# Bias rows reversed by a diagonal DMA, late probabilities scaled on either engine, longer GpSimd memsets: one layer of a streaming encoder

## The chip, the cores and the metric

The kernel runs on one core of one Trainium2 chip. The core has five engines that run side by side and meet through semaphores: TensorE (PE in the profile; PEld is its weight load), VectorE (DVE), ScalarE (ACT), GpSimd (POOL) and SyncE (SP), which here issues the DMAs. Each engine works through its own instructions strictly in order. The metric is the device time of one execution in microseconds, given as the median of several runs.

## The reference

One layer of an encoder runs on 2048 new frames of a prompt and on 64 frames of a running stream, with rows of 1024 numbers, all in 32-bit floats. Half of the width is chunked attention in 8 heads of 64, the other half a gated linear recurrence in 4 heads of 128.

```python
def band_attention(q, k, v, rel, valid, rel_bias):
    idx = jnp.clip(rel, -REL_CLIP, REL_CLIP) + REL_CLIP
    bias = rel_bias[:, idx].astype(jnp.float32)
    s = jnp.einsum('bnqhd,bnkhd->bnhqk', q, k).astype(jnp.float32) * ATTN_SCALE + bias
    s = jnp.where(valid[None, :, None], s, NEG_INF)
    p = jax.nn.softmax(s, axis=-1).astype(v.dtype)
    return jnp.einsum('bnhqk,bnkhd->bnqhd', p, v)

def mixer_layer(x, ln_g, w_in, lb, norm_g, w_out, attn_fn, s0):
    B, T, _ = x.shape
    aq, ak, av, ag, hq, hf, hi, hg = jnp.split(rms_norm(x, ln_g) @ w_in, SPLITS, axis=-1)
    heads = lambda a: a.reshape(B, T, H_A, DH_A)
    k = heads(ak)
    v = heads(av)
    o_a = attn_fn(heads(aq), k, v).reshape(B, T, W_A) * jax.nn.silu(ag)
    o_b, S = hgrn2_branch(hq, hf, hi, hg, lb, norm_g, s0)
    y = x + jnp.concatenate([o_a, o_b], axis=-1) @ w_out
    return y, k, v, S
```

The bias depends only on the distance between query and key, clipped to 128 either way. For 128 queries against 640 keys the matrix of biases therefore has one constant part (384 keys, all further than 128 back) and one part of 256 keys whose rows are the same list of 383 numbers, each row shifted by one against the row above.

## The kernel before

The frames are handled in four superblocks (`SUPER`) of 512, 576, 512 and 512 tokens; the second has the 64 frames of the running stream. In each superblock 32 projections of 128 columns run (`JOBS`), each as 24 matmuls on high and low halves of the operands. The heads hang on these: a pair of attention heads needs its projections pq, pk, pv, pg, a recurrent head hq, hf, hi, hg. After the last superblock the output projection follows (`steps`), with seven products of half-size blocks for each 256 rows.

The order of all instructions is made when the program is built. A class `Plan` keeps a clock for every engine; `Queue` charges each instruction with a cost in ns as it is issued; generators (threads) yield a time, an engine with a time, or a condition, and are resumed when the plan's clock says so, those of lower priority number first. `yield "D", t` means: go on when time t has come and VectorE's line in the plan is less than 600 ns long. Tokens (`tk[...]`) stand for buffers. `C.pick(t, D=..., A=...)` names the engine on which an operation of the given cost would end first. A DMA on SyncE is charged 420 ns of issue, 520 ns until it moves, its bytes at 370 GB/s behind the DMAs before it, and 2000 ns until it has landed; `C.dma()` adds 100.

Three places matter here.

*The breath.* Where GpSimd gets a third instruction in a row while its line in the plan is not empty, `Queue` puts a memset of the tile `C.breath` ahead of it. In the kernel before this tile has one element per partition.

*The bias rows,* `load_bias`. One tile `bias` of 128 x 2 x 640 (two heads of a pair) exists; the pair's scores are added to it by VectorE. In superblocks 1 to 3 it is loaded from a copy in DRAM (`biasd`). In superblock 0 it is built, once for each of the four pairs: a DMA loads a window `win` in which partition i holds the 256 numbers from place i of the list on (into the tile `ck`), a second DMA loads the far value; VectorE fills the 384 constant columns; TensorE multiplies with `flip`, a matrix with ones on the other diagonal, which turns the order of the 128 partitions round; VectorE takes the product out of the bank `g` with a factor of -1; two memsets mask the corners; a DMA stores the result to `biasd`. `d.bias_at` is the planned time from which scores of the pair may go.

*The probabilities,* `softmax_exp`. ScalarE exponentiates a row block of scores and sums it, VectorE takes the reciprocal, and the block is scaled by it: on VectorE, but on ScalarE once "parts" is in `have`. That is set in `out_rows_g`, when the recurrences of the last superblock are done and the output projection has room to begin, so it concerns the last scores alone.

TensorE then transposes the scaled blocks; ScalarE copies them out as high halves, VectorE makes the low halves (`ph`), and TensorE multiplies them with v (`pv`).

Of the kernel before, what the change touches and what calls it, by code (L numbers as in the profile page):

```python
# [8 lines left out]
F32 = mybir.dt.float32  # L9
# [3 lines left out]
ALU = mybir.AluOpType  # L13
# [4 lines left out]
P = 128  # L18
D = 1024
# [353 lines left out]
def hymba_step(  # L373
# [24 lines left out]
    C = Plan()  # L398
    act, dve, pool, pe, sp = (Queue(C, e, x) for e, x in (("A", nc.scalar), ("D", nc.vector), ("P", nc.gpsimd),
                                                          ("T", nc.tensor), ("S", nc.sync)))  # L400
# [4 lines left out]
    cst = ctx.enter_context(tc.tile_pool(name="cst", bufs=1))  # L405
    wk = ctx.enter_context(tc.tile_pool(name="wk", bufs=2))
    dr = ctx.enter_context(tc.tile_pool(name="dr", bufs=1, space=DRAM))
# [5 lines left out]
    def T(pool_, shape, dt, tag, **kw):  # L413
        uid[0] += 1
        C.name(homes.get(id(pool_), ""), tag, kw.get("bufs") or 1, f"{tag}_{uid[0]}")
        return pool_.tile(list(shape), dt, tag=tag, name=f"{tag}_{uid[0]}", **kw)

    def psum(tag, shape=(P, 512), bufs=1):
        return T(ps, shape, F32, tag, bufs=bufs)
# [22 lines left out]
    def mm32(out, w, x):  # L442
        pe.matmul(out, w, x, start=True, stop=True)

    tk = {k: Tok(C, n) for k, n in dict(acc=2, s_ps=1, tr=2, pv=1, g=1, pr=PRB, ph=2, sig=2, vT=2, mixa=2,
                                     w=WBUFS, raw=RAWB, xn=XNB, kv=1, q=1, sga=2, bias=1, gf=1, gi=1, gg=1,
                                     ck=1, slot=4, x4=0, x5=0, rec=1).items()}
# [1 line left out]

    ident = T(cst, [P, P], F32, "ident")  # L450
    make_identity(nc, ident)
    flip = T(cst, [P, P], F32, "flip")
    ones = T(cst, [P, P], F32R, "ones")
    mask = T(cst, [P, P], U32, "mask")
    eps_t = T(cst, [P, 1], F32, "eps")
    one_t = T(cst, [P, 1], F32, "one")
    C.breath = T(cst, [P, 1], F32, "breath")
    reset = T(cst, [P, 512], F32, "reset")
    asb = [T(cst, [P, 4, P], F32, f"asb{i}") for i in range(2)]
    g_norm = T(cst, [P, NHB], F32, "gnorm")  # L460
# [5 lines left out]
    have = set()  # L466

    def constants():
        pool.memset(eps_t, EPS)
        pool.memset(one_t, 1.0)  # L470
        maskf = asb[0][:, 0]
        pool.memset(maskf, 1.0)
        dve.tensor_copy(ones, maskf)
        pool.memset(flip, 1.0)
        pool.affine_select(out=flip, in_=flip, pattern=[[1, P]], compare_op=ALU.is_equal, fill=0.0,
                           base=-(P - 1), channel_multiplier=1)
        pool.affine_select(out=maskf, in_=maskf, pattern=[[1, P]], compare_op=ALU.is_ge, fill=0.0,
                           base=0, channel_multiplier=-1)
        dve.tensor_copy(mask, maskf)
        pool.memset(reset, 1.0)  # L480
        pool.memset(reset.rearrange("p (b t) -> p b t", t=32)[:, :, 0:1], 0.0)
        pool.memset(asb[0], 0.0)
# [333 lines left out]
    def load_bias(sb, p, d):  # L816
        yield from tk["bias"].get()
        nb = d.bias = T(wk, [P, 2, 640], F32, "bias", bufs=1)
        if sb:
            sp.dma_start(nb, biasd[p])  # L820
            d.bias_at = C.dma(655)
            return
        yield from tk["ck"].get()
        win = T(wk, [P, 4, P], F32, "ck", bufs=1).rearrange("p (h a) c -> p h (a c)", h=2)
        sp.dma_start(win, bass.AP(rel_rev.tensor, 2 * p * 383, [[1, P], [383, 2], [1, 256]]))
        far = T(wk, [P, 2], F32, "far", bufs=1)
        sp.dma_start(far, bass.AP(rel_rev.tensor, 2 * p * 383, [[0, P], [383, 2]]))
        t = C.dma(400)
        yield "D", t
        for h in range(2):  # L830
            dve.tensor_scalar(nb[:, h, 0:384], reset[:, :384], 0.0, far[:, h : h + 1], ALU.mult, ALU.subtract)
        C.dve(600)
        yield from tk["g"].get()
        pw = psum("g")
        pe.matmul(pw, flip, win.rearrange("p h c -> p (h c)"), start=True, stop=True)
        tk["ck"].put()
        t = C.pe()
        yield "D", t
        dve.tensor_scalar(nb[:, :, 384:640], pw.rearrange("p (h c) -> p h c", h=2), -1.0, None, ALU.mult)
        tk["g"].put(1, C.dve())  # L840
        dve.memset(nb[64:128, :, 0:64], BIG)
        dve.memset(nb[0:64, :, 576:640], BIG)
        t = C.dve(900, t)
        d.bias_at = t
        yield t
        sp.dma_start(biasd[p], nb)
        C.dma(655)
# [38 lines left out]
    def pair_jobs(sb, p):  # L886
# [10 lines left out]
        def open_():  # L897

            yield from tk["kv"].get()
            d.kd = T(pa, [P, 2, WIN + NMAX], F32R, "kd")  # L900
            d.v = T(pa, [P, 9, 4, 64], F32R, "v")
            d.q = T(pa, [P, 2, QW], F32R, "q")
            if sb:
                cd = carry[sb - 1][p]
                sp.dma_start(f32(d.kd[:, :, 0:512]), cd[:, 0:2, :])
                sp.dma_start(f32(d.v[:, 0:4].rearrange("p t s d -> p (t s d)")),
                             cd[:, 2:4, :].rearrange("p a c -> p (a c)"))
                d.k_t = d.v_t = C.dma(1024)
            C.spawn(load_bias(sb, p, d), 1)
            if smp:  # L910
                pool.memset(f32(d.v[DEC:, 4 + WIN // P]), 0.0)
                C.spawn(sample_cache(d), 1)
# [98 lines left out]
    def softmax_rows(d, h, qc, spans, bcol, nk, out):  # L1011

        yield lambda: d.q_n >= qc + P and d.k_n >= qc + P and d.bias_at is not None
        yield max(d.q_t, d.k_t, d.bias_at) + 300.0
        yield from tk["s_ps"].get()
        yield from tk["pr"].get()
        sps = s_ps()
        for part in (d.q, ql):
            for i, (k0, kn) in enumerate(spans):
                mm(sps[:, i, :kn], part[:, h, qc : qc + P], d.kd[:, h, k0 : k0 + kn], kn,  # L1020
                   start=part is d.q, stop=part is ql)
        t = C.pe()
        yield "D", t
        s = T(wk, [P, 640], F32, "pr", bufs=PRB)
        nm = T(wk, [P, 2], F32, "nm", bufs=4)
        ns, kn = len(spans), spans[0][1]
        dve.tensor_tensor_reduce(
            s[:, :nk].rearrange("p (a c) -> p a c", a=ns), sps[:, :ns, :kn],
            d.bias[:, h, bcol : bcol + nk].rearrange("p (a c) -> p a c", a=ns),
            1.0, 3e38, ALU.add, ALU.min, nm[:, 0:1])  # L1030
        t = C.dve(nk + 80, t)
        tk["s_ps"].put(1, t)
        d.left -= 1
        if d.left == 0:
            if d.sb == len(SUPER) - 1 and d.p == NPAIR - 1:
                have.add("scores")
                tk["x4"].put()
            tk["bias"].put()
        yield "A", t
        yield from softmax_exp(s, nm, nk, out, t)  # L1040

    def softmax_exp(s, nm, nk, out, t):
        sm = T(wk, [P, 1], F32, "sm", bufs=4)
        act.activation(s[:, :nk], s[:, :nk], AF.Exp, bias=nm[:, 0:1], scale=-1.0, accum_out=sm)
        t = C.act(nk + 300, t)
        yield "D", t
        dve.reciprocal(sm, sm)
        t = C.dve()
        if "parts" in have:
            yield "A", t  # L1050
            act.activation(s[:, :nk], s[:, :nk], AF.Copy, scale=sm)
            t = C.act()
        else:
            dve.tensor_scalar(s[:, :nk], s[:, :nk], sm, None, ALU.mult)
            t = C.dve()
        out.append((s, t))
# [184 lines left out]
    def sample_a(d, c0, marks):  # L1241
# [41 lines left out]
        yield "A", t  # L1283
        out = []
        yield from softmax_exp(s, nm, 576, out, t)
        pr, t = out[0]
        yield lambda: marks[-1]["pv"] and turn["ph"] == turn["given"]
# [749 lines left out]
    def program():  # L2037


        dve.memset(g_in, 0.0)  # L2040
        constants()
        kroom = f32(T(pa, [P, 2, WIN + NMAX], F32R, "kd")).rearrange("p a c -> p (a c)")
        vroom = f32(T(pa, [P, 9, 4, 64], F32R, "v")).rearrange("p t s d -> p (t s d)")
# [252 lines left out]
```

## Time and profile before

| | us |
|---|---|
| median of 3 runs | 1261.63 |
| lowest, highest | 1260.84, 1261.96 |
| the profiled execution, its own time | 1260.86 |
| its span, first to last instruction | 1259.0 |
| in this span: ScalarE's wait for projections (vT, sig) | 95.5 and 73.3 |
| GpSimd's longest wait (mixa for VectorE) | 259.6 |
| HBM traffic | 215 GB/s over the span |

Most of the span is projection: the groups of matmuls with more time than all others are these (columns: line, engine and operation, output and inputs, shapes, count, then busy us and mean ns of one, then the idle time just before them).

```profile
L266 PE MATMUL acc<-xh,w 128*128 128x512 f32 (+2 forms) x2720 | 568.4, 348 | 1.0 <-ACT sig L266 0.8
L266 PE MATMUL acc<-xl,w 128*128 128x512 f32 (+2 forms) x1360 | 297.4, 348 | 0.0
L266 PE MATMUL pv<-ph,v 128*128 128x256 f32 (+2 forms) x344 | 97.2, 373 | 3.1 <-DVE ph L266 2.4
```

All instructions carry line 266, because a helper records them; groups are told apart by the names of their tiles. Durations of matmuls overlap, so busy time is their union and not count times mean. A view by stretches gives the busy time of every engine in each stretch of the span; the timeline gives instructions in order of time, with their start, length and, in brackets, how long the engine had been idle before and what ended that.

### The profile page before, as it was taken

What the parts mean: (1) busy time and instruction counts of PE and PEld (TensorE: products, weight loads), DVE (VectorE), ACT (ScalarE), POOL (GpSimd) and SP (SyncE); (2) the same over time, 40 slices, a digit from 0 to 9 for tenths busy, and PEclk for the clock granted to TensorE, in tenths of its full rate; (3) what the DMA queues carried; (4) which work ended last, traced back from release to release, by engine and by line L of the source; (5) the groups of instructions that cost most, each with busy time, mean ns of one, the idle gap of its engine ahead of it and who ended that gap; (6) DMA issues with size and microseconds to landing.
All of it is one profiled execution on the core that took longest, in us unless ns stands there. A gap on an engine that the chain in (4) does not pass through costs nothing. (4 is left out here: it accounts for less than half of the span.)

```text
span 1259.0 us, 22201 instructions
## 1 busy us (share of the span) xinstructions
PE 1238.8 (98%) x8120; PEld 1081.6 (86%) x8120; DVE 891.9 (71%) x1854; ACT 706.9 (56%) x1548; POOL 379.9 (30%) x703
## 2 busy tenths in 40 slices
PE   9999999999999999999999999999999999999997
PEld 8788887999999999998888888998888888788786
DVE  7786968766857678686584849783838574578886
ACT  6453546665656557575565656764636454753443
POOL 7766655111120210202533634110101104451110
PEclk9999999999999999999999999999999999999999
DMA  7887787645354554636879597646454657886331
GB/s 288 301 288 244 247 282 281 219 168 202 138 188 142 181 200 144 216 125 236 272 248 303 206 364 254 220 164 210 144 212 136 222 178 279 324 277 203 126 134 67
DMA packets 94830, 271.72 MB, mean 216 GB/s; under 512 B 10305, under 2 KB 43073, under 8 KB 77058
## 3 DMA queue, kind: packets, MB, share of 16 engines
q1 hardware_dynamic: 94722, 270.31, 61.4%
q8 instruction: 64, 1.05, 0.3%
q14 instruction: 44, 0.36, 0.1%
HBM read 186.66 MB, written 83.62 MB: 215 GB/s over the span
## 5 line engine op out<-in xcount | busy, mean ns | idle before, releaser
L266 PE MATMUL acc<-xh,w 128*128 128x512 f32 (+2 forms) x2720 | 568.4, 348 | 1.0 <-ACT sig L266 0.8
L266 PEld LDWEIGHTS acc<-xh,w 128*128 128x128 f32 x2720 | 436.7, 189 | 51.7 <-issue 1.4
L266 PE MATMUL acc<-xl,w 128*128 128x512 f32 (+2 forms) x1360 | 297.4, 348 | 0.0
L266 PEld LDWEIGHTS acc<-xl,w 128*128 128x128 f32 x1360 | 219.3, 189 | 24.9 <-issue 0.5
L266 POOL TENSOR_TENSOR mixa<-mixa,sga 128x256 f32<-128x256 f32 (+1 forms) x36 | 29.8, 828 | 334.8 <-DVE mixa L266 259.6
L266 DVE CUSTOM_DVE_ANT_0 pr<-s,bias 128x640 f32<-128x640 f32 (+5 forms) x144 | 100.7, 703 | 34.5 <-PE s L266 33.9
L266 ACT ACTIVATE pr<-pr,nm 128x640 f32<-128x640 f32 (+4 forms) x132 | 100.7, 763 | 39.0 <-DVE nm L266 37.9
L266 ACT CAST ph<-tr 128x512 fp32r<-128x512 f32 (+3 forms) x176 | 88.1, 507 | 59.7 <-PE tr L266 27.9
L266 POOL TENSOR_TENSOR w<-wraw,w 128x256 fp32r<-128x256 f32 x120 | 105.3, 906 | 46.9 <-DVE w L266 25.9
L266 DVE TENSOR_TENSOR ph<-tr,ph 128x512 fp32r<-128x512 f32 (+3 forms) x176 | 101.1, 589 | 10.0 <-ACT ph L266 8.8
L266 PE MATMUL pv<-ph,v 128*128 128x256 f32 (+2 forms) x344 | 97.2, 373 | 3.1 <-DVE ph L266 2.4
L266 PE MATMUL tr<-ident,pr 128*128 128x128 f32 x580 | 91.2, 273 | 2.4 <-DVE pr L266 1.2
L266 PEld LDWEIGHTS tr<-ident,pr 128*128 128x128 f32 x580 | 70.4, 140 | 16.6 <-issue 3.8
L266 ACT ACTIVATE sig<-acc 128x256 f32<-128x256 f32 (+2 forms) x86 | 42.7, 497 | 73.6 <-PE acc L266 73.3
L266 ACT COPY vT<-acc 128x512 f32<-128x512 f32 (+2 forms) x64 | 31.3, 488 | 71.2 <-PE acc L266 71.1
L266 DVE TENSOR_SCALAR pr<-pr,sm 128x640 f32<-128x640 f32 (+3 forms) x124 | 67.9, 547 | 4.4
L266 DVE TENSOR_TENSOR mixa<-mixa,pv 64x256 f32<-64x256 f32 (+1 forms) x144 | 56.8, 394 | 18.9 <-ACT mixa L266 14.7
L266 PEld LDWEIGHTS pv<-ph,v 128*128 128x128 f32 x344 | 57.4, 190 | 10.3 <-issue 2.0
L266 ACT ACTIVATE sig<-sig 128x512 f32<-128x512 f32 (+2 forms) x109 | 57.3, 528 | 10.0 <-DVE gk L266 7.3
L266 PE MATMUL s<-kd,q 128*128 128x320 f32 (+3 forms) x232 | 56.9, 315 | 0.2
L266 POOL TENSOR_TENSOR xn<-wraw,xn 128x256 fp32r<-128x256 f32 x48 | 37.8, 803 | 62.2 <-ACT xn L266 62.1
L266 PE MATMUL s<-kd,ql 128*128 128x320 f32 (+3 forms) x232 | 55.6, 309 | 0.0
(319 smaller groups left out, 2064.5 us busy)
## 6 DMA issues: line engine op xcount, KB each, us to landing
w<-wd SPq DMA_DIRECT2D x96, 1024.0 KB, 5.1
wd<-w SPq DMA_DIRECT2D x32, 1024.0 KB, 7.6
wraw<-in_w_in_dram SPq DMA_DIRECT2D x30, 512.0 KB, 5.5
wod<-xn SPq DMA_DIRECT2D x28, 512.0 KB, 5.0
xn<-in_x_prompt_dram SPq DMA_DIRECT2D x23, 512.0 KB, 5.5
bias<-biasd SPq DMA_DIRECT2D x12, 640.0 KB, 7.5
carry<-kd SPq DMA_DIRECT2D x12, 512.0 KB, 8.0
carry<-v SPq DMA_DIRECT2D x12, 512.0 KB, 5.2
```

What stands on the lines that cost most here:

```text
L266: r = f(*args, **kw)
```

## The change

The tile `flip`, its memset and its selection on GpSimd go. The tile `breath` grows from one element per partition to 128.

In `load_bias` the window, the matmul, the bank `g` and the tile `ck` go. In their place a DRAM tile `rel{p}` of 2 x 128 x 383 is filled by one DMA from DRAM to DRAM that repeats each of the two lists of 383 numbers 128 times. When the plan's clock says that it has landed, a second DMA reads it back into columns 384 to 640 of the bias tile with a step of 382 from partition to partition, so that each partition starts one place earlier in the list: that is the reversed order. VectorE then negates these columns in place. The constant columns are filled between the two.

In `softmax_exp` the late blocks go to ScalarE only where `C.pick` finds that it would end there sooner than on VectorE.

```diff
-    flip = T(cst, [P, P], F32, "flip")
...
-    C.breath = T(cst, [P, 1], F32, "breath")
+    C.breath = T(cst, [P, P], F32, "breath")
...
-        pool.memset(flip, 1.0)
-        pool.affine_select(out=flip, in_=flip, pattern=[[1, P]], compare_op=ALU.is_equal, fill=0.0,
-                           base=-(P - 1), channel_multiplier=1)
...
-        yield from tk["ck"].get()
-        win = T(wk, [P, 4, P], F32, "ck", bufs=1).rearrange("p (h a) c -> p h (a c)", h=2)
-        sp.dma_start(win, bass.AP(rel_rev.tensor, 2 * p * 383, [[1, P], [383, 2], [1, 256]]))
+        same = T(dr, [2, P, 383], F32, f"rel{p}")
+        sp.dma_start(same, bass.AP(rel_rev.tensor, 2 * p * 383, [[383, 2], [0, P], [1, 383]]))
+        t = C.dma(400)
         far = T(wk, [P, 2], F32, "far", bufs=1)
         sp.dma_start(far, bass.AP(rel_rev.tensor, 2 * p * 383, [[0, P], [383, 2]]))
+        C.dma()
+        yield t
+        near = nb[:, :, 384:640]
+        sp.dma_start(near, bass.AP(same.tensor, same.offset + P - 1, [[382, P], [383 * P, 2], [1, 256]]))
         t = C.dma(400)
-        yield "D", t
+        yield "D", C.now
         for h in range(2):
             dve.tensor_scalar(nb[:, h, 0:384], reset[:, :384], 0.0, far[:, h : h + 1], ALU.mult, ALU.subtract)
-        C.dve(600)
-        yield from tk["g"].get()
-        pw = psum("g")
-        pe.matmul(pw, flip, win.rearrange("p h c -> p (h c)"), start=True, stop=True)
-        tk["ck"].put()
-        t = C.pe()
         yield "D", t
-        dve.tensor_scalar(nb[:, :, 384:640], pw.rearrange("p (h c) -> p h c", h=2), -1.0, None, ALU.mult)
-        tk["g"].put(1, C.dve())
+        dve.tensor_scalar(near, near, -1.0, None, ALU.mult)
...
-        if "parts" in have:
+        if "parts" in have and C.pick(t, D=680.0, A=780.0) == "A":
             yield "A", t
             act.activation(s[:, :nk], s[:, :nk], AF.Copy, scale=sm)
```

## The prediction

> **What bounds the kernel now.** I read the page first, the table of busy times above all.
>
> ```profile
> span 1259.0 us, 22201 instructions
> PE 1238.8 (98%) x8120; PEld 1081.6 (86%) x8120; DVE 891.9 (71%) x1854; ACT 706.9 (56%) x1548; POOL 379.9 (30%) x703
> ```
>
> TensorE is busy for all but 1259.0 - 1238.8 = 20.2 us. So an edit pays in one of two ways: it takes work away from TensorE, or it closes one of the gaps that make up these 20.2 us. Work on the other engines counts only where TensorE waits for it. Next I read busy time by stretches of 50 us (columns: stretch, length, then busy us and instruction count of TensorE's matmuls, weight loads, VectorE, ScalarE, GpSimd, then granted clock, DMA share and GB/s), to see where the gaps lie; the last row but one is from the same view in steps of 5 us.
>
> ```profile
> 0.00:50.00 50.00, 45.38 (x326) 38.95 (x327) 37.68 (x62) 26.47 (x55) 36.28 (x71) 1.00 0.80 292
> 150.00:200.00 50.00, 48.39 (x294) 39.66 (x294) 36.50 (x71) 23.26 (x49) 28.65 (x39) 1.00 0.83 288
> 1050.00:1100.00 50.00, 47.63 (x241) 39.74 (x240) 24.64 (x52) 30.08 (x58) 24.14 (x40) 1.00 0.89 336
> 1085.00:1090.00 5.00, 4.96 (x22) 3.70 (x20) 0.95 (x4) 5.00 (x11) 2.46 (x5) 1.00 1.00 405
> sum 1250.00, PE 1236.37 PEld 1079.91 DVE 888.08 ACT 704.50 POOL 379.89; mean PE 49.45 PEld 43.20 DVE 35.52 ACT 28.18 POOL 15.20
> ```
>
> Of the gaps, 1250.00 - 1236.37 = 13.6 us lie before 1250 us and 20.2 - 13.6 = 6.6 in the tail. Inside, 50.00 - 45.38 = 4.6 belong to the start, so 9.0 us are spread over the middle; 2.37 of them fall into 1050 to 1100 us, the stage that the late edit touches, and 1.61 into one of the stretches in which bias rows are built. The granted clock is 1.00 throughout, so it is no part of the question.
>
> **Bias rows: TensorE's share.** The reversing matmul (flip times window) goes, four times. Its records are two per matmul:
>
> ```profile
> 107.74 1.02 PE L266 MATMUL g<-ck,flip 128*128 128x512 f32 x2
> 108.20 1.03 PE L266 MATMUL acc<-xh,w 128*128 128x512 f32 x2
> 109.07 1.53 PE L266 MATMUL acc<-xl,w 128*128 128x512 f32 x6
> 111.04 0.70 PE L266 MATMUL g<-q,ones 128*128 128x512 f32 x2 [0.44 <-DVE bias L266]
> 111.58 0.62 PE L266 MATMUL acc<-xl,w 128*128 128x512 f32 x2
> 112.04 2.20 PE L266 MATMUL acc<-xh,w 128*128 128x512 f32 x9
> 169.14 0.70 PE L266 MATMUL g<-q,ones 128*128 128x512 f32 x2 [0.44 <-DVE bias L266]
> ```
>
> Durations of pipelined matmuls overlap, so I price by starts. Two ordinary 512-column matmuls take 112.04 - 111.58 = 0.46 us. From the first flip record to the matmuls two places on it takes 109.07 - 107.74 = 1.33. The flip therefore costs 1.33 - 0.46 = 0.87 us of TensorE's line, and four cost **-3.5 us**. Nothing covers this: TensorE has work before and behind each of them. In addition TensorE waited twice 0.44 us for VectorE to empty the flip's bank, so that the normalizing matmul could have it. Without the flip that bank isn't taken; the wait goes whole (-0.9) or the matmul finds its own operand late (0). I take **-0.5**.
>
> **Bias rows: the new transfers.** One DMA of 256 KB (the window) becomes two in series: a DRAM-to-DRAM copy of 2 x 128 x 383 x 4 = 392 KB, and a 256 KB read back along the diagonal, which can start only when the copy has landed. SyncE issues three DMAs per pair instead of two. No row shows a DRAM-to-DRAM transfer, so I bound it.
>
> ```profile
> ck<-in_rel_bias_dram SPq DMA_DIRECT2D x4, 256.0 KB, 4.2
> wraw<-in_w_in_dram SPq DMA_DIRECT2D x30, 512.0 KB, 5.5
> carry<-kd SPq DMA_DIRECT2D x12, 512.0 KB, 8.0
> 96.31 0.43 SPq L266 DMA_DIRECT2D ck<-in_rel_bias_dram  x1
> 98.93 0.34 SPq L266 DMA_DIRECT2D wraw<-in_w_in_dram  x1
> 102.48 0.33 SPq L266 DMA_DIRECT2D wraw<-in_w_in_dram  x1
> ```
>
> From below it is 4.2 us (the smaller read), from above 8.0 (the larger store); by size it is nearest to the 5.5 of a 512 KB read, which I take. The read back has the window's size and takes 4.2. Counted from the first issue it lands at 5.5 + 0.4 (an issue, 0.43) + 4.2 = 10.1 us, range 8.8 to 12.6. The program's own clock puts it earlier: 520 + 392/370 x 1000 + 2000 + 100 = 3.7 us for the copy and 520 + 708 + 2000 + 100 = 3.3 for the read, 7.0 together. So VectorE can meet its negation about 10.1 - 7.0 = 3.1 us early, in order, with everything behind it: bank evacuations, weight casts, recurrence products. SyncE too stands still for up to 5.5 - 3.7 = 1.8 us before the read back; after the second pair's window that is from 100.0 to 101.8, and its next load in the rows is at 102.48, so nothing queues behind it. What queues behind VectorE:
>
> ```profile
> 104.98 0.69 DVE L266 CAST w<-wraw 128x1024 fp32r<-128x1024 f32 x1 [0.63 <-PE acc L266]
> 107.03 0.69 DVE L266 TENSOR_TENSOR sga<-acc,sig 128x512 f32<-128x512 f32 x1 [1.35 <-ACT sig L266]
> 109.60 0.69 DVE L266 TENSOR_TENSOR q<-k,q 128x512 fp32r<-128x512 f32 x1 [1.88 <-POOL k L266]
> 123.15 0.19 PEld L266 LDWEIGHTS s<-kd,q 128*128 128x128 f32 x1
> 237.20 0.34 SPq L266 DMA_DIRECT2D biasd<-bias  x1
> 237.69 0.19 PEld L266 LDWEIGHTS s<-kd,q 128*128 128x128 f32 x1
> ```
>
> If VectorE stands from 104.4 to 106.4, the cast and one evacuation come up to 2 us late, and the idle 1.35 and 1.88 us behind them absorb it before the operand at 109.60 that TensorE takes next. The rows themselves have time: the first scores that use them start at 123.15, 16.7 us after 106.4. The first and third pair look the same. The fourth has no such room: its rows were done at 237.20 and its first scores followed at 237.69, so scores and what VectorE does around them move by the 2 to 3 us. TensorE has projections to put there. I take 1.0 us lost on TensorE for that pair and nothing for the others: **+1.0**, between 0 (all hidden) and 4 x 3.1 = 12.4 (all exposed). By the Trainium skill, "DMA: Bandwidth & Descriptors", Anatomy of one DMA, a transfer takes about 2.0 us plus its bytes at 436 GB/s, which would land the two by about 5.9 us, an estimate; VectorE would never wait and this term would be 0. The trace speaks against it: the 256 KB read has 4.2 us, not 2.6.
>
> **Longer memsets and the removed constants.**
>
> ```profile
> L266 POOL MEMSET breath<- x36: 88/98/642, 23.0 to 1112.7; 128x1 f32 x36
> L266 POOL MEMSET flip<- x1: 204/204/204, 1.5 to 1.5; 128x128 f32 x1
> L266 POOL TENSOR_SCALAR_AFFINE_SELECT flip<-flip x1: 423/423/423, 1.8 to 1.8; 128x128 f32<-128x128 f32 x1
> PE g L266 <- POOL one L266: 1.4, 1, 1.4
> 8.07 1.04 POOL L266 CAST w<-wraw 128x1024 fp32r<-128x1024 f32 x1 [4.48 <-DMA wraw<-in_w_in_dram]
> ```
>
> A memset of the new shape is in the trace by chance: 204 ns against 98. That is 36 x 0.106 = 3.8 us more on GpSimd, which is idle 70% of the span; a longer opening may let a waiting VectorE operation in. In the table of waits TensorE waited for GpSimd once, 1.4 us for the first constants, and nowhere later, so I take **0**, between -1 and +3.8. By the Trainium skill, "SBUF — State Buffer", Who interferes with whom, a two-port VectorE operation (a cast, a scaling) is shut out by any GpSimd instruction for its whole length: the longer memsets would then cost VectorE up to the 3.8 us, and give room only to its two-input operations. The pool's flip constants (0.2 + 0.4 us) are covered by the 4.48 us that GpSimd then waits for its first weights: 0.
>
> **Late probabilities.** Eight rows, from 1071 us on, are scaled on ScalarE.
>
> ```profile
> L266 ACT ACTIVATE pr<-pr,sm x8: 813/830/833, 1071.1 to 1100.5; 128x640 f32<-128x640 f32 x8
> L266 DVE TENSOR_SCALAR pr<-pr,sm 128x640 f32<-128x640 f32 x88 | 51.2, 582 | 3.1
> 1077.95 0.60 ACT L266 COPY asb<-acc 128x512 f32<-128x512 f32 x1
> 1078.58 0.69 DVE L266 TENSOR_TENSOR xn<-xn,acc 128x512 f32<-128x512 f32 x1 [1.61 <-ACT asb L266]
> 1080.02 0.70 PE L266 MATMUL pv<-ph,v 128*128 128x512 f32 x2 [0.96 <-DVE ph L266]
> 1086.88 1.54 ACT L266 ACTIVATE pr<-pr,sm 128x640 f32<-128x640 f32 x2
> 1090.20 0.69 DVE L266 TENSOR_TENSOR xn<-xn,acc 128x512 f32<-128x512 f32 x1 [2.66 <-ACT asb L266]
> 1090.80 1.01 DVE L266 TENSOR_TENSOR ph<-tr,ph 128x256 fp32r<-128x256 f32 x2
> 1091.37 0.48 PE L266 MATMUL pv<-ph,v 128*128 128x256 f32 x2 [1.41 <-DVE ph L266]
> ```
>
> One scaling takes 0.83 us on ScalarE and 0.58 on VectorE. Both gaps of TensorE in this stage end at a low half (ph) that VectorE made late; VectorE was late because the operation ahead of it waited for a copy (asb) on ScalarE, and that copy stood behind scalings: one of 0.83 before the gap of 0.96, two in 1.54 us before the gap of 1.41. Between 1085 and 1090 ScalarE was busy for 5.00 of 5 us and VectorE for 0.95. The new choice takes the engine that would end first, with 680 for VectorE against 780 for ScalarE; with such loads that is VectorE nearly always. Then the copies come 0.83 and 1.54 us sooner, and of the gaps 0.96 - 0.83 = 0.1 and nothing are left: a gain of 0.83 + 1.41 = 2.2 us at most. VectorE pays 8 x 0.58 = 4.7 us, in a stretch of which it is idle half. What is late next is the residual addition on VectorE, which a scaling can now stand before (0.58). I take **-1.7**, between -2.4 (both gaps) and 0.
>
> **The sum** is -3.5 - 0.5 + 1.0 + 0 - 1.7 = -4.7 us. The profiled execution took 1260.86 us itself, 1.9 more than its span, so the changed kernel's would take 1256.2; the median of the runs shown, 1261.63, is 0.8 above that execution, and so is my forecast for the median: **1257.0 us**.
>
> One thing no row prices: instructions are issued in the order in which the program's own clock finds them ready, and four matmuls less, other due times for the bias and other costs shift that clock from the first pair on. The 9.0 us of gaps in the middle will lie elsewhere afterwards. I allow 2 us either way for it.
>
> **Rivals.** (a) *The late scaling brings nothing*, because the choice keeps ScalarE, or the waits pass to the residual additions. For it: VectorE's low half, evacuations and additions stand in one queue. Against: 0.95 of 5 us. Time: 1257.0 + 1.7 = 1258.7. That the choice doesn't do what it says is part of this.
>
> (b) *The gaps take it back.* The order shifts, and half as much again as the 9.0 us of gaps appears elsewhere, 4.5 us: 1261.5, no change. For it: eight rows of scores and all projections are placed by the same clock. Against: no stretch of the middle but the two shown has more than about 1 us of gap, so the order hides most delays now.
>
> (c) *Slower: VectorE stands at the negation, and TensorE behind it.* One mechanism, in the four places where bias rows are built: the read back lands 3.1 us after the program thinks, VectorE blocks in order, and TensorE's next recurrence product or bank is late by as much. If all of it comes through, 12.4 us, with the other terms -5.7: 1261.6 + 6.7 = 1268.3; with two thirds of it, 8.3, it is 1264.2. It decides from 5.7 / 4 = 1.4 us lost per pair on. For it: VectorE waited for the loads of the bias rows in the kernel before, too. Against: the idle time behind the place in the second pair, 1.35 + 1.88 us, and scores that come 16.7 us later.
>
> (d) *The longer memsets cost what they last*: their 3.8 us reach TensorE through VectorE's casts. Time: 1257.0 + 3.8 = 1260.8, no change. Against: of 36 memsets few fall where VectorE's next result is awaited. This is the outcome that the Trainium skill's rule on the shared port would give at its worst.
>
> **How the numbers follow.** A difference under 0.2%, 2.5 us, can't be told from none here, so "faster" means under 1259.1 and "slower" over 1264.1. Forecast 0.55, (a) 0.14, (b) 0.14, (c) 0.13, (d) 0.04. The forecast with its 2 us either way is 1255.0 to 1259.0, all of it faster but for 0.02; (a) gives 0.09 faster and 0.05 the same; (b) gives 0.01 faster, 0.10 the same and 0.03 slower; (c) gives 0.02 the same and 0.11 slower; (d) is the same. Together: faster 0.63, same 0.23, slower 0.14. The range goes down to the sum with every term at its good end: -3.5 - 0.9 - 2.4 = -6.8 and 2 us of order, 1252.8. Upwards it takes in (a), (b), (d) and (c) with two thirds exposed, to 1264.2.
>
> **What would show it.** TensorE has 8 records of flip fewer and its busy time is 3 to 4 us lower: if it isn't, the first term is wrong. The copy and the read back land 5.5 and 4.2 us after issue: if VectorE's idle time before its negation exceeds 3 us a pair and TensorE has gaps at 40 to 50, 103 to 108, 161 to 166 and 236 to 242 us, (c) is right. In the last attention TensorE's gaps before pv shrink from 0.96 and 1.41 us to under 0.5 and six or more of the eight scalings stand on VectorE: if they do stand there and the gaps stay, (a). If all this is as I say and the median stays within 2.5 us of 1261.63, the gaps have moved, (b), and the stretches of 50 us must show where.

## The result and the profile after

The changed kernel takes 1270.24 us (median of 6 runs, 1267.1 to 1271.77), beside 1261.8 (6 runs, 1260.84 to 1263.05) for the kernel before: a ratio of 1.0064 with a 95% interval of 1.0051 to 1.0077, or 8 us slower. The forecast was 1257.0, its range ended at 1264.2. The profiled execution took 1269.01 us; the numbers below are from it. First the page's table of busy times, after:

```profile
span 1267.0 us, 22172 instructions
PE 1238.7 (98%) x8112; PEld 1086.4 (86%) x8112; DVE 890.1 (70%) x1865; ACT 700.7 (55%) x1540; POOL 369.7 (29%) x698
```

The 8 records of the reversing matmul are gone (8120 to 8112), yet TensorE is busy as long as before, 1238.7 against 1238.8 us, and its gaps (the span less the busy time) have grown from 20.2 to 28.3 us. Where they lie is told by the loads and stores of the bias tile (the tile's own view: count, shortest, median and longest ns of an issue, then the start of the first and of the last). Before:

```profile
L266 SPq DMA_DIRECT2D bias<-biasd x12: 422/432/640, 279.5 to 1048.8; - x12
L266 SPq DMA_DIRECT2D bias<-in_x_prompt_dram x3: 332/454/2482, 1096.4 to 1202.5; - x3
```

and after, with what VectorE waited for at this tile (us, times) below it:

```profile
L266 SPq DMA_DIRECT2D bias<-biasd x12: 416/436/816, 293.8 to 1061.9; - x12
L266 SPq DMA_DIRECT2D bias<-in_x_prompt_dram x3: 333/494/2563, 1108.8 to 1211.8; - x3
...
  DMA far<-in_rel_bias_dram: 31.9, 4
  DMA bias<-rel: 0.5, 2
```

The first row of each starts when the bias is first reloaded, that is behind superblock 0; the second when the last attention is over. So the span falls into three stretches:

| stretch | before | after | difference |
|---|---|---|---|
| to the first reload (superblock 0, bias rows built) | 279.5 | 293.8 | +14.3 |
| to the load behind the last attention | 816.9 | 815.0 | -1.9 |
| to the end (output projection) | 162.6 | 158.2 | -4.4 |

All of the loss lies where bias rows are built; the rest of the kernel gained 6.3 us. And one wait stands out there: VectorE stood 31.9 us in all, in four waits, for `far`, the far values of 1 KB, and almost nothing (0.5) for the read back. Transfers in the view of DMA issues (count, KB of one, median us from issue to landing):

```profile
rel<-in_rel_bias_dram SPq DMA_DIRECT2D x4, 383.0 KB
...
bias<-rel SPq DMA_DIRECT2D x4, 256.0 KB, 4.3
...
far<-in_rel_bias_dram SPq DMA_DIRECT2D x4, 1.0 KB, 12.1
```

The read back took 4.3 us, where 4.2 were forecast. The 1 KB took 12.1. The timeline shows why, for the first pair and, from 101.20 on, for the second:

```profile
36.48 0.76 SPq L266 DMA_DIRECT2D rel<-in_rel_bias_dram  x1
37.29 5.78 SPq L266 DMA_DIRECT2D far<-in_rel_bias_dram  x1
...
47.65 1.98 PE L266 MATMUL acc<-xl,w 128*128 128x512 f32 x8
...
49.46 1.98 PE L266 MATMUL acc<-xh,w 128*128 128x512 f32 x8
...
52.66 0.38 SPq L266 DMA_DIRECT2D bias<-rel  x1
52.86 0.75 DVE L266 TENSOR_SCALAR bias<-reset,far 128x384 f32<-128x384 f32 x2 [8.29 <-DMA far<-in_rel_bias_dram]
...
54.74 0.69 DVE L266 TENSOR_TENSOR sga<-acc,sig 128x512 f32<-128x512 f32 x1
...
55.49 3.02 PE L266 MATMUL acc<-xh,w 128*128 128x512 f32 x8 [4.05 <-DVE sga L266]
...
58.30 2.73 PE L266 MATMUL acc<-xl,w 128*128 128x512 f32 x8
...
101.20 0.65 SPq L266 DMA_DIRECT2D rel<-in_rel_bias_dram  x1
101.90 2.52 SPq L266 DMA_DIRECT2D far<-in_rel_bias_dram  x1
...
113.91 0.38 SPq L266 DMA_DIRECT2D bias<-rel  x1
114.04 0.75 DVE L266 TENSOR_SCALAR bias<-reset,far 128x384 f32<-128x384 f32 x2 [7.69 <-DMA far<-in_rel_bias_dram]
```

SyncE can issue the read back only when the copy has landed: 52.66 - 36.48 = 16.2 us after it, and 12.7 in the second pair. `far` was issued right behind the copy and set VectorE free at 52.86, within 0.2 us of it, in the second pair again (113.91, 114.04). So `far` landed with the copy: the 12.1 us are the second pair's, and in the first it took 15.6. VectorE had then stood 8.29 us in front of the constant columns; the evacuation behind them (sga) frees the bank that TensorE needs, and TensorE stood 4.05. In all TensorE waited most for VectorE (us in all, times, longest):

```profile
PE acc L266 <- DVE sga L266: 6.2, 2, 4.1
PE g L266 <- DVE q L266: 4.7, 2, 3.5
```

Busy times by stretches (columns as in the prediction; the last row is for later):

```profile
44.00:46.00 2.00, 2.00 (x12) 1.75 (x13) 0.57 (x1) 1.31 (x3) 1.30 (x2) 1.00 0.13 42
...
52.00:56.00 4.00, 0.51 (x2) 0.47 (x3) 2.71 (x5) 1.30 (x3) 1.21 (x2) 1.00 0.59 176
56.00:60.00 4.00, 4.00 (x12) 3.12 (x12) 3.22 (x8) 0.00 (x0) 2.43 (x4) 0.57 1.04 345
...
0.00:300.00 300.00, 282.06 (x1806) 241.97 (x1807) 217.00 (x434) 154.17 (x334) 147.92 (x244) 0.97 0.70 251
...
1062.00:1112.00 50.00, 49.49 (x253) 41.70 (x252) 30.11 (x64) 28.36 (x58) 26.76 (x44) 1.00 0.91 337
```

Three things stand here. While the copy ran alone (first row) the DMA share was 0.13, as much as 2 of 16 engines fully busy, at 42 GB/s. Behind the gap the granted clock fell to 0.57 for a while, so the gap costs more than its length. And over the first 300 us TensorE has 17.9 us of gaps and a mean clock of 0.97, where the kernel before had 7.8 us in 280 and a clock of 1.00:

```profile
0.00:280.00 280.00, 272.20 (x1774) 232.00 (x1775) 217.52 (x429) 150.25 (x324) 151.76 (x239) 1.00 0.73 257
```

Gaps +10.1, the clock 0.03 x 300 = about 9, less the 3.5 that the reversing matmul was priced at: +15.6, near the 14.3 of the table.

### The profile page after: what moved, and what is told of

It reads as the page before. It is cut to its first block, busy times and chain, and to the rows that moved or that the text cites. A ratio compares the mean times of both kernels' runs of the same rounds, so it can differ in the third digit from the quotient of the medians.

```text
span 1267.0 us, 22172 instructions
## 1 busy us (share of the span) xinstructions
PE 1238.7 (98%) x8112; PEld 1086.4 (86%) x8112; DVE 890.1 (70%) x1865; ACT 700.7 (55%) x1540; POOL 369.7 (29%) x698
## 4 chain that ended last, share of the span: by engine, by line
PE 80%; DVE 4%; DMA 3%; issue 2%; ACT 1%; POOL 1%; SPq 0%; DVEq 0%; ACTq 0%; POOLq 0%
PE acc L266 58%; PE g L266 6%; PE tr L266 6%; PE s L266 5%; PE pv L266 5%; DMA wraw<-in_w_in_dram 2%; DMA far<-in_rel_bias_dram 1%; DVE xn L266 1%; POOL w L266 0%; DVE pr L266 0%; POOL pf L266 0%; DVE mixa L266 0%; DVE kd L266 0%; DVE q L266 0%; DVE w L266 0%
## 5 line engine op out<-in xcount | busy, mean ns | idle before, releaser
L266 POOL TENSOR_TENSOR w<-wraw,w 128x256 fp32r<-128x256 f32 x120 | 101.5, 874 | 66.5 <-DVE w L266 51.1
L266 PEld LDWEIGHTS tr<-ident,pr 128*128 128x128 f32 x580 | 71.1, 140 | 14.5 <-issue 2.8
L266 DVE TENSOR_SCALAR pr<-pr,sm 128x640 f32<-128x640 f32 (+4 forms) x132 | 74.8, 567 | 4.7
L266 DVE TENSOR_TENSOR mixa<-mixa,pv 64x256 f32<-64x256 f32 (+1 forms) x144 | 56.8, 395 | 20.2 <-ACT mixa L266 15.9
L266 POOL TENSOR_TENSOR k<-ob 128x512 f32<-128x512 f32 (+2 forms) x20 | 18.2, 910 | 129.2 <-ACT ob L266 119.2
```

The source lines that it names most:

```text
L266: r = f(*args, **kw)
```

## The experiments

All ratios are to the kernel before, run beside it on the same chip. The three edits were first taken apart.

**The old bias rows in the new kernel.**

```diff
-        same = T(dr, [2, P, 383], F32, f"rel{p}")
-        sp.dma_start(same, ...)
+        yield from tk["ck"].get()
+        win = T(wk, [P, 4, P], F32, "ck", bufs=1).rearrange("p (h a) c -> p h (a c)", h=2)
...
+        pe.matmul(pw, flip, win.rearrange("p h c -> p (h c)"), start=True, stop=True)
```

> The changed kernel with the bias rows built as before (window, reversing matmul, bank g); the long memsets and the choice of engine for the late probabilities stay. Theory A (the bias rows' copy from DRAM to DRAM is the loss: VectorE waits some 8 us four times for the far value that landed behind it): the loss goes and the late gain stays, 1256 to 1261 us; the gaps of TensorE between 40 and 250 us are as small as before, 7 to 8 us in the first 250 us against 17.9 in the changed kernel. Rival B (the long memsets or the choice of engine upset the order): it stays at 1266 us or more.

1254.8 us, 0.9949 (0.9932 to 0.9966), a little below what was expected. With the flip and its window back, the other two edits gain some 6 us. The new bias rows therefore cost 1.0064 - 0.9949 = 0.0115, 14.5 us, inside the changed kernel.

**The new bias rows alone in the kernel before** (the same lines of `load_bias` and the constant, nothing else).

> The kernel before with the new bias rows alone (short memsets, late probabilities always on ScalarE). Theory A: all of the loss and none of the late gain, 1269 to 1275 us. Rival B: 1257 to 1263 us.

1278.34 us, 1.0129 (1.0106 to 1.0151), above the 1269 to 1275 expected, with VectorE waiting 29.5 us for `far` in four waits. The loss is in this edit, from either side.

**The copy with the 128 rows outermost.** Two things could make the copy slow: that it goes from DRAM to DRAM and is as large as it is, or the order in which it is written, two lists outermost.

```diff
-        same = T(dr, [2, P, 383], F32, f"rel{p}")
-        sp.dma_start(same, bass.AP(rel_rev.tensor, 2 * p * 383, [[383, 2], [0, P], [1, 383]]))
+        same = T(dr, [P, 2, 383], F32, f"rel{p}")
+        sp.dma_start(same, bass.AP(rel_rev.tensor, 2 * p * 383, [[0, P], [383, 2], [1, 383]]))
...
-        sp.dma_start(near, bass.AP(same.tensor, same.offset + P - 1, [[382, P], [383 * P, 2], [1, 256]]))
+        sp.dma_start(near, bass.AP(same.tensor, same.offset + P - 1, [[765, P], [383, 2], [1, 256]]))
```

> The changed kernel, with the copy laid out with the 128 rows outermost and the two heads inside (128 x 2 x 383 in place of 2 x 128 x 383), and the read back along the diagonal of that layout. The same bytes, the same number of pieces. Theory A1 (the copy is slow because its outermost count is 2, so that it runs on few of the 16 DMA engines; their share was 0.18 while it ran alone): it lands in 4 to 7 us in place of 13 to 16, far within 5 us, VectorE's wait for far falls from 31.9 to under 6 us in all, and the time to 1254 to 1260 us. Rival A2 (128 reads of one place in DRAM, or DRAM to DRAM at all, are slow): the copy still takes over 10 us, and the time stays at 1266 to 1272 us.

1249.3 us, 0.9909 (0.9887 to 0.9931): the same bytes between the same memories, and 0.0155 (19.6 us) less than the changed kernel. It beats both kernels, and by more than was expected. Its view of DMA issues, and one of its 50-us stretches:

```profile
rel<-in_rel_bias_dram SPq DMA_DIRECT2D x4, 383.0 KB, 7.0
...
far<-in_rel_bias_dram SPq DMA_DIRECT2D x4, 1.0 KB, 6.0
```

```profile
150.00:200.00 50.00, 50.00 (x305) 41.70 (x304) 40.96 (x78) 28.75 (x61) 31.70 (x42) 1.00 0.83 307
```

The copy lands in 7.0 us instead of 12.7 to 16.2, `far` in 6.0 instead of 12.1, and TensorE has no gap left between 150 and 200 us, where it had 1.61 us in the kernel before. VectorE still waits 4.1 us for `far`, in three waits, without harm.

**The order alone.** That version changed the layout of the DRAM tile too. Here the layout of the changed kernel stays and only the copy is written in another order:

```diff
-        sp.dma_start(same, bass.AP(rel_rev.tensor, 2 * p * 383, [[383, 2], [0, P], [1, 383]]))
+        sp.dma_start(bass.AP(same.tensor, same.offset, [[383, P], [P * 383, 2], [1, 383]]),
+                     bass.AP(rel_rev.tensor, 2 * p * 383, [[0, P], [383, 2], [1, 383]]))
```

> The changed kernel; the copy fills the same 2 x 128 x 383 tile in the same places, but its access is written with the 128 rows outermost on both sides. Theory A1 (the outermost count of the access decides how many DMA engines share the copy): it lands in 5 to 8 us as with the other layout, VectorE's wait for far is under 6 us in all, 1246 to 1252 us. Rival A3 (the layout in DRAM decides, the two heads' rows lying 196 KB apart): 12 to 16 us and 1266 us or more.

One run, 1247.22 us. VectorE waits 7.3 us for `far`, more than the 6 expected at most. In its view of DMA issues:

```profile
rel<-in_rel_bias_dram SPq DMA_DIRECT2D x4, 383.0 KB, 7.4
...
far<-in_rel_bias_dram SPq DMA_DIRECT2D x4, 1.0 KB, 6.7
```

The order of the access patterns makes the difference, not the layout: the bytes, the memories and the places are those of the changed kernel. This is as the Trainium skill has it: by "DMA: Bandwidth & Descriptors", Why a DMA increments its semaphore by 16 and not by 1, a transfer runs on as many engines, up to 16, as divide the slowest dimension of both its sides: 2 for [2, 128, 383], 16 for 128 rows outermost. The trace agrees with its share of 0.13.

**Far values ahead of the copy.** Is the loss only that 1 KB sits behind the copy?

```diff
+        far = T(wk, [P, 2], F32, "far", bufs=1)
+        sp.dma_start(far, bass.AP(rel_rev.tensor, 2 * p * 383, [[0, P], [383, 2]]))
         same = T(dr, [2, P, 383], F32, f"rel{p}")
```

> The changed kernel with the far value's DMA issued ahead of the copy. Theory A: the copy still takes 13 to 16 us, so VectorE no longer waits for far but meets its negation before the read back has landed and waits there as long; 1265 to 1273 us. Rival C (only the place of the far value behind the copy costs, the negation has time): VectorE's waits for the bias rows fall under 6 us in all and the time is 1256 to 1262 us.

1276.14 us, 1.011 (1.0082 to 1.0138): no gain, rather worse, and not by the wait that was expected. VectorE's wait for `far` is gone, and at the negation it waits only 6.3 us in three waits, against 31.9 for `far` in the changed kernel. TensorE still waits for VectorE, 6.0 us for `sga` in two waits and 3.4 for `stp` in one. The table of waits by the bias tile, then SyncE's (us in all, times, longest):

```profile
  DMA bias<-rel: 6.3, 3
```

```profile
SPq L266 <- DMA rel<-in_rel_bias_dram: 29.3, 4, 7.5
```

Where VectorE stands now is told by the timeline:

```profile
42.51 0.46 SPq L266 DMA_DIRECT2D wraw<-in_w_in_dram  x1
...
51.50 0.38 SPq L266 DMA_DIRECT2D bias<-rel  x1
...
52.83 0.69 DVE L266 CAST w<-wraw 128x1024 fp32r<-128x1024 f32 x1 [7.38 <-DMA wraw<-in_w_in_dram]
...
114.90 0.69 DVE L266 CAST w<-wraw 128x1024 fp32r<-128x1024 f32 x1 [8.81 <-PE acc L266]
...
178.57 0.69 DVE L266 CAST w<-wraw 128x1024 fp32r<-128x1024 f32 x1 [8.05 <-issue]
```

The weights (`wraw`) that are loaded behind the copy are now about as late as the copy. In the first pair their load is issued at 42.51, the copy has landed by 51.50, when the read back goes out, and VectorE, which has stood 7.38 us for the weights, casts them at 52.83. In the second and third pair it stands 8.81 and 8.05 us at the same cast, until 0.8 and 1.3 us behind the issue of the read back (114.08 and 177.30). The view names other causes there, so that it is the load in these pairs too is inferred from the moment. SyncE stands 29.3 us for the copy (24.7 in the changed kernel, its row is below). So it is the copy's length that costs, whichever wait shows it. Why the time is even longer than the changed kernel's was not found.

**Far values ahead of the quick copy.** The same move in the version with 128 rows outermost.

> The version with the rows outermost, with far issued ahead of the copy. VectorE waited 4.1 us in all for far behind the copy there, while TensorE had no gap between 100 and 250 us. So: VectorE's waits for far go to under 1 us, and the time stays within 1 us of that version (1249.3), since TensorE waited for none of it. If it is faster by more than 1.5 us, those waits did reach TensorE.

1250.01 us, 0.9905 (0.9892 to 0.9919), the same as without the move. VectorE waits nothing for `far` and 1.4 us for the read back. Once the copy is quick the order of the two issues is worth nothing that can be measured, as expected.

**All four copies at the start.** With the quick copy, all four are issued at 20 us, so that no pair has to wait for one.

```diff
+            for p in range(NPAIR):
+                sp.dma_start(rel[p], bass.AP(rel_rev.tensor, 2 * p * 383, [[0, P], [383, 2], [1, 383]]))
...
-        yield t
```

> The version with the rows outermost, with all four copies issued together some 15 us into the kernel, when the first weights are split, so that each pair needs only far and the read back. Theory G (what is left of the cost is VectorE's 4.1 us of waiting for far behind the copy and the read back's lateness): VectorE's waits for the bias rows fall to under 1.5 us and the time by 0 to 3 us, to 1246 to 1249.5 us. Rival H (with rows outermost all of it is hidden, and four copies at the start, 3 MB of traffic, hold up the first weights): 1249 to 1254 us.

1260.37 us, 0.9978 (0.9968 to 0.9988), 0.0069 (8.7 us) more than with each copy in its place. From its timeline:

```profile
20.09 4.01 SPq L266 DMA_DIRECT2D rel<-in_rel_bias_dram  x4
...
46.45 0.75 DVE L266 TENSOR_SCALAR bias<-reset,far 128x384 f32<-128x384 f32 x2 [7.66 <-DMA far<-in_rel_bias_dram]
```

and its stretch in between:

```profile
28.00:44.00 16.00, 16.00 (x74) 13.02 (x72) 9.95 (x10) 6.35 (x12) 12.19 (x26) 1.00 0.99 369
```

This is slower than either side expected. The DMA engines are full (0.99) from 28 to 44 us, and the first pair stands for `far` as in the changed kernel, although no copy of its own is ahead of it. That the 1.5 MB of copies pushed the loads of the start together is the likely reason; no row follows it through. I had not seen that the start has no room in its transfers.

**The late scaling alone.** Its edit is the one line with `C.pick`.

> The kernel before with the choice of engine for the late probabilities alone. Both other parts together with it, without the new bias rows, gave 5.9 us. Theory D (the late choice is most of this: it closes the two gaps of 0.96 and 1.41 us and lets the order of the last stage move up): 3.5 to 6 us faster than before, 1254.5 to 1257.5 us; TensorE's gaps in 1050 to 1100 us fall from 2.4 to under 0.7. Rival E (the long memsets are most of it): within 1.5 us of before.

1260.06 us, 0.9986 (0.9975 to 0.9998), a gain of 1.7 us. All eight late scalings went to VectorE, and the stretch that had 47.63 us of TensorE now has

```profile
1050.00:1100.00 50.00, 48.93 (x247) 41.08 (x246) 30.30 (x62) 28.38 (x57) 25.41 (x43) 1.00 0.90 330
```

That this edit makes most of the 6 us of the first experiment (D) is wrong; the memsets are left for the larger part.

**The longer memsets alone.** Its edit is the size of the tile `breath`.

> The kernel before with the long memsets alone. Theory D: within 1.5 us of before, 1259 to 1262 us; GpSimd's 36 or so memsets last 0.1 us longer and TensorE waits for none. Rival E: 3 us or more faster. Rival F (longer memsets shut VectorE out): 1 to 4 us slower.

1258.32 us, 0.9965 (0.9951 to 0.9979), a gain of 4.4 us where I had put 0. A larger tile also moves every tile behind it in SBUF, so the next kernel takes the two apart.

**The larger tile, the old memset.** The order of instructions is that of the kernel before; the memset writes one element of a tile with 128, and the tiles behind it lie 480 bytes further on.

```diff
-    C.breath = T(cst, [P, 1], F32, "breath")
+    C.breath = T(cst, [P, P], F32, "breath")[:, 0:1]
```

> The kernel before with the longer tile for the memsets, but memsets of one element per partition as before: every instruction and its order is that of before, only most SBUF tiles lie 480 bytes further on. With long memsets the kernel was 4.4 us faster, and in the output projection three matmuls took 0.68 us from start to start of the next three in place of 0.70, from first to last and whatever ran beside them. Theory P (the places of the operands set that pace, not the memsets): 0.68 here too, the stage from the first residual load to the end 160 to 161.5 us against 162.6, and 1.5 to 4.5 us faster than before. Rival M (the memsets' length does it): pace 0.70, within 1 us of before.

1261.1 us, 0.9991 (0.9982 to 0.9999): a gain of 1.1 us, without one longer memset. It is less than the places were expected to bring, and its interval all but reaches 1. In the output projection the matmuls became quicker, and that stage takes 160.4 us against 162.6; the rest is 1.7 us longer. The tile view of `acc`, before and then here (count, shortest, median and longest ns):

```profile
L266 PE MATMUL acc<-xh,slot x96: 391/396/398, 1097.9 to 1243.5; 128*128 128x512 f32 x96
```

```profile
L266 PE MATMUL acc<-xh,slot x96: 387/389/399, 1099.6 to 1243.1; 128*128 128x512 f32 x96
```

So of the 4.4 us some 1.1 goes with the place and 0.0026 of the ratio, 3.3 us (about 2 either way, from the two intervals), with the memsets' length.

**Both again on the quick copy.** First a pad that puts the tiles behind `breath` back to their old places modulo 512 bytes, with the long memsets; then the larger tile with the short ones.

```diff
+    T(cst, [P, 8], F32, "pad")
```

> The version with the rows outermost, with 32 bytes of padding behind the long memset tile, which puts the tiles of the projections back on the places they had before the change; the long memsets and the order of instructions stay. Theory P: the pace of three matmuls in the output projection goes back to 0.70 us, the stage from the first residual load to the end from 158.2 to 160 to 161 us, and the whole takes 1.5 to 4.5 us more than without the padding (that took 1249.3). Rival M: 0.68, 158.2 and within 1 us of it.

1252.17 us, 0.9921 (0.9905 to 0.9937); the matmul's record is 396 ns again.

```diff
-    C.breath = T(cst, [P, P], F32, "breath")
+    C.breath = T(cst, [P, P], F32, "breath")[:, 0:1]
```

> The version with the rows outermost, with the long tile and its places but memsets of one element per partition. Theory P: pace 0.68, within 1.5 us of that version (1249.3). Rival M: 2 to 5 us slower than it, 1251.5 to 1254.5 us.

1251.35 us, 0.9913 (0.9899 to 0.9927), with 389 ns. The matmul's pace follows the place in every kernel, but the two times lie within each other's intervals and within that of the quick copy with both, 0.9909 (their medians, 2.9 and 2.1 us above that version's, were taken on another chip). Here, then, the memsets' length is worth no more than can be measured. What it was worth on the old order, 3.3 us, is inconclusive as to its cause: in the kernel before with the larger tile, TensorE's gaps in the first 250 us are 6.2 us with the long memsets and 8.5 with the short ones, and no row tells which wait the memset takes away.

## Why the prediction was wrong

**The step that failed** is the price of the copy: "From below it is 4.2 us (the smaller read), from above 8.0 (the larger store); by size it is nearest to the 5.5 of a 512 KB read, which I take." It took 12.7 to 16.2 us, and the far values, issued behind it, landed with it. The price went by bytes, and the rows that it was taken from all have 128 partitions outermost; the copy has 2. With 128 outermost it takes 7.0 to 7.4, which the bounds would have held. At the 42 GB/s that the trace shows while it ran alone, its 392 KB take 9.3 us, an estimate; what other transfers on those two engines add was not measured apart. By "DMA: Bandwidth & Descriptors", Anatomy of one DMA, of the Trainium skill, two engines of sixteen at its 436 GB/s in all would need 7.2 + 2.0 = 9.2 us, an estimate too. The Trainium skill gives that sum for transfers that GpSimd issues, and these are issued by SyncE; the prediction set the sum beside its own price and did not ask for the number of engines.

**The term of the new transfers,** +1.0 between 0 and 12.4, was therefore far out: with the rest of the bias rows at -4.0 and the whole at +14.5, it is +18.5. Its upper end rested on a VectorE 3.1 us early in each pair; it stood 8 us per pair.

**Rival (c)** had the right mechanism, VectorE standing in order and TensorE behind it, and the wrong place: the constant columns, not the negation. Its price, 1268.3 us with all of it exposed, was still 2 us short. The prediction never asked when the far values, issued behind the copy, would land; the row of 12.1 us for 1 KB is the answer. The idle 1.35 and 1.88 us that spoke against the rival were too small for a wait of 7.69 in that pair. What no term had is the clock of 0.57 behind a gap. SyncE's wait, priced at up to 1.8 us with nothing queued behind it, was up to 7.4 in the changed kernel (us in all, times, longest), and its issue of `far` behind the copy, priced at 0.4 us, took 5.78 and 2.52 us in the rows above (0.6 to 1.1 behind the quick copy), so the next weights went out later too:

```profile
SPq L266 <- DMA rel<-in_rel_bias_dram: 24.7, 4, 7.4
```

Rivals (a) and (b) did not come: the late scaling brought its share, and the gaps did not wander but grew where the bias rows are built.

**The flip.** -3.5 and -0.5 fit what was measured, though they were not measured apart: with the quick copy the new bias rows gain 0.9949 - 0.9909 = 0.0040, 5.0 us (about 3.5 either way, from the two intervals), where the sum had -3.0. The sign named for this term, TensorE's busy time 3 to 4 us lower, failed in the changed kernel (1238.7 against 1238.8), where the mean clock was 0.992 instead of 0.999. With the quick copy, at 0.999, it is 1230.4 us, against 1236.4 in the first experiment, which has the other two edits and the flip, at 0.998.

**Memsets,** put at 0: -4.4 by themselves, outside the -1 to +3.8. The memset takes about what the row said, 202 ns:

```profile
L266 POOL MEMSET breath<- x39: 194/202/207, 22.6 to 1121.2; 128x128 f32 x39
```

No cost shows, as argued; the gain was not foreseen. Part of it is the place of other tiles, which I did not see in a change of a tile's size. Rival (d), that they cost what they last, did not come.

**Late scaling,** -1.7: measured -1.7 by itself (0.3 to 3.2, from the interval). In the changed kernel this stage lies 12.4 us later; in 1062 to 1112 us (its row is above) TensorE has 0.51 us of gaps where it had 2.37, the wait for ph before pv fell from 2.4 us in two to 0.5 in one, and all scalings are VectorE's:

```profile
L266 DVE TENSOR_SCALAR pr<-pr,sm x132: 286/553/1079, 70.6 to 1110.4; 128x640 f32<-128x640 f32 x96, 128x128 f32<-128x128 f32 x8, 128x256 f32<-128x256 f32 x8, 128x384 f32<-128x384 f32 x8
```

**The sum again:** the new bias rows +14.5 (flip and bank at their forecast -4.0, the transfers the rest, +18.5), memsets -4.4, scaling -1.7 make +8.4, near the result of 8. The split inside the bias rows is not measured. Two checks are: the bias rows alone cost 0.0129 (16.3 us) in the kernel before against 0.0115 (14.5) in the changed one, and memsets and scaling one by one gain 6.1 us, against some 6 together.

## What to carry to other kernels

Price a transfer by the outermost count of both access patterns before its bytes: two lists outermost kept 383 KB on 2 of 16 engines, and exchanging two dimensions was worth 19.6 us. In this kernel a transfer issued behind a slow one was about as late as that one, 1 KB of far values or 512 KB of weights, and the engine that waited for it in order passed the wait on; moving the small one ahead did not help, because the next load stood behind the slow one instead. A tile of another size moves the tiles behind it, so a control keeps the places and changes the use.

## What the hardware showed that was not expected

*The clock.* After TensorE had been idle for 4.05 us, the granted clock was 0.57 over the next stretch of 4 us; eight matmuls took 49.46 - 47.65 = 1.81 us from start to start ahead of the gap and 58.30 - 55.49 = 2.81 behind it. By the Trainium skill, "TensorE: Matmul & The Clock Gate", Part 1: The HAM clock gate, the array runs at half clock until it has been busy for about 3.4 us; 0.57 over 4 us is (1 - 0.57) x 4 / 0.5 = 3.4 us at half, which agrees. In steps of half a microsecond the clock was 1.00 up to 56.0 us, 0.92 in the next step and 0.50 from 56.5 to 59.5: the half clock set in some 0.9 us after the matmuls had resumed at 55.49, not with them.

*The place of operands.* Three matmuls of 512 columns in the output projection follow each other in 0.70 us with the tiles where the kernel before has them, and in 0.68 when they lie 480 bytes further on in their partition. From the timeline before, and from that of the larger tile with the old memset:

```profile
1135.36 0.63 PE L266 MATMUL acc<-xh,slot 128*128 128x512 f32 x2
...
1136.06 0.63 PE L266 MATMUL acc<-xh,slot 128*128 128x512 f32 x2
```

```profile
1136.83 0.61 PE L266 MATMUL acc<-xh,slot 128*128 128x512 f32 x2
...
1137.51 0.61 PE L266 MATMUL acc<-xh,slot 128*128 128x512 f32 x2
```

All runs fall in line: the record's median is 396 ns before, with the late scaling alone, the new bias rows alone and the pad, and 389 in those with the tiles moved, whatever the length of the memsets. Which tile it is, and why its place matters, was not tried.
